# Hymba streaming step on one core: attention values as a two-part product, the first half of the output product placed between attention tiles, and an earlier order of the second state-space group

## Chip, core and metric

One core of a Trainium2 chip. The metric is device microseconds (us) of one execution of the whole two-layer step; lower is better. The engines are TensorE (PE in the rows, with its weight loads as PEld), VectorE (DVE), ScalarE (ACT), GpSimd (POOL) and SyncE (SP, which issues the DMAs).

## Reference

Each of two layers computes, for 1024 prompt tokens and 64 sample tokens, `h = RMSNorm(x)`, one combined projection `h . W_in`, three branches (A: a gated linear recurrence; B: attention over the top keys of an indexer; C: a Mamba-2 state-space scan in two groups), and `x + W_out . concat[y_A, y_B, y_C]`. All of it is float32. The part that matters here is B's tail and the output product:

```python
    p = jax.nn.softmax(logits, axis=-1)
    o = jnp.einsum('bqgrk,bqkgd->bqgrd', p.astype(vsel.dtype), vsel)
...
    y_b = o * jax.nn.silu(ga)
...
    mix = jnp.concatenate([y_a, y_b, y_c], axis=-1)
    x = x + jnp.einsum('bte,ed->btd', mix, p['w_out'].astype(mix.dtype)).astype(x.dtype)
```

The kernel masks the keys that the indexer did not choose instead of gathering the chosen ones, so the softmax and the product with V run over all keys up to the query's tile.

## The kernel before, in words

**Numbers in two parts.** Most products are made of float32 split into a high part (type fp32r) and a low part (the rest): `three` (lines 212 to 217) makes hi.hi, hi.lo and lo.hi, one matmul per part and per 128 rows of depth. `split` (188 to 194) makes the parts of a 128x1024 weight block: ScalarE the high, VectorE or GpSimd the low.

**Attention** (966 to 1122). Work is cut into 18 tiles per layer, list `todo` (1110): a tile of 128 queries (64 for tile 8, the sample tokens) for one of two key-value groups of four heads. Tile t < 8 sees 128(t+1) keys; tile 8 sees 576. The loop at 1115 starts the queries of tile i+2, the weights of tile i+1 and the values of tile i. `weigh` (1038) per head: two matmuls per 512 keys (1068), VectorE adds mask and bias while it takes a running extreme (1071), ScalarE takes the exponential with its sum (1075), VectorE the reciprocal (1077) and the normalized weights (1078). `values` (1081) per block of 128 keys: four transposes of the weights into one bank (1093), a ScalarE copy to `pT` (1095), and for each pair of heads a float32 matmul with 64 columns of V (1098) into the one bank `s1`; at the end VectorE multiplies with the gate (1100) and two DMAs write `ybd` (1102). A layer has 82 such blocks: 72 of 128 queries and 10 of tile 8.

**Output product.** `out_proj` (956 to 964) goes over eight blocks d of 128 output rows; each has three chunks of columns, 24 matmuls a chunk. Its first half (1127) needs `yad` and the first state-space group and no attention; it is written after the attention loop in the program, and it is what TensorE has to do beside attention. Its second half (1161, 1165) needs `ybd`: chunks 0 and 1 hold tokens of tiles 0 to 5, chunk 2 those of tiles 6 to 8. `y_tile` (942) loads a piece and splits it; line 1158 does so for all three chunks before line 1161.

**Order.** The framework lays out a fixed order for every engine from the order of the program and a simulated clock; an engine then runs its list in order. Work later in the program has lower priority and fills gaps. `PLAN` (22) is a list written by hand of projections (x, z, a, q, l, g) and steps of the two state-space groups (s0, s1); `run(PLAN[3])` at 927 and `steps(g[1])` at 928 end the stage before attention. Each s1 is one tile of the second group (`ssd`, 747); after its last tile come token sums, a norm (817) and the write of `ycd` (819). l and g are the recurrence blocks and their gates.

**Memory.** The attention's constant tiles (`kst`, `vt`, `nb`, `ks`) lie where the state-space pools lay and wait until those are free; then `nb` (971), `vt` (980 to 982) and `ks` (988) are loaded by SP, in order. Two banks `tp` hold transposes, three `mm` the output product, one `s1` the values.

Of the kernel before, what the change touches and what calls it, by code (L numbers as in the profile page):

```python
# [20 lines left out]
DEPTH = 2  # L21
PLAN = ('', 'X8 x10 z2 x1 x0 z3 x2 x3 s0 x9 s0 z4 s0 x11 s0 z5 s0 z6 s0 x4 s0 X5 s0 z7 s0 s0 X6 x7', 's0 s1 a0 q1 s0 q0 s1 a1', 's1 s1 q3 q2 s1 l0 s1 g0 s1 l1 g1 s1 s1 l2 g2 s1 l3 s1 g3', 'a3 a2')
RAW = 2
# [14 lines left out]
TS = 64  # L38
# [44 lines left out]
def body(ctx, tc, I, O):  # L83
# [36 lines left out]
    def s1_bank():  # L120
        return bank("s1", 1)
# [42 lines left out]
    def softplus(out, x, n, tag, sign=1.0, where=None):  # L164
# [16 lines left out]
        V.scalar_tensor_tensor(out, q, 2.0, z, op0=OP.mult, op1=OP.add)  # L181

    def load(block):
        raw = wts.tile([128, 1024], F32, name="wraw", bufs=RB)
        SP.dma_start(raw, block)
        return raw

    def split(raw, eng):

        hi = wts.tile([128, 1024], F32R, name="whi")  # L190
        lo = wts.tile([128, 1024], F32R, name="wlo")
        S.activation(hi, raw, AF.Copy)  # L192
        eng.tensor_tensor(lo, raw, hi.bitcast(F32), op=OP.subtract)  # L193
        return hi.rearrange("p (k c) -> p k c", k=8), lo.rearrange("p (k c) -> p k c", k=8)
# [84 lines left out]
    for l in range(DEPTH):  # L279
# [675 lines left out]

        def out_proj(half, Y, chunks, done, eng=G):

            for d in range(8):
                ws = weights(I["w_out"][l, half, d], eng)
                for ci in chunks:  # L960
                    a, b = CH[ci]
                    ps = mm_bank()
                    three(ps[:, :b - a], ws, Y, ci)
# [15 lines left out]

        SP.dma_start(vt[:, 0:8, :], kvd[:, 0:8, 128:256])  # L980
        SP.dma_start(vt[:, 8:12, :], I["cache_att_v"][l])
        SP.dma_start(vt[:TS, 12, :], kvd[:TS, 8, 128:256])
        kf, kc_ = [p.tile([128, 1024], F32, name="lg", bufs=8) for _ in range(2)]
# [5 lines left out]
        def keys(g, t0, w):  # L989

            n = TS if t0 == 12 else 128
            kb_ = (ks_ if t0 == 12 else kf)[:n, t0 % 12:t0 % 12 + w, 64 * g:64 * g + 64][:, :, None, :].to_broadcast([n, w, 2, 64])
            khl = p.tile([128, 2, 4, 64], F32R, name="pT")
            S.activation(khl[:n, :w, 0:2, :], kb_, AF.Copy)
# [43 lines left out]
        def weigh(t, g, qst):  # L1038
# [15 lines left out]
            for h in range(4):  # L1054
# [22 lines left out]
                V.reciprocal(ri[:nq, h:h + 1], sm[:nq, h:h + 1])  # L1077
                V.tensor_scalar(lg[:nq, :nk], lg[:nq, :nk], ri[:nq, h:h + 1], None, op0=OP.mult)  # L1078
            return lgs

        def values(t, g, lgs):

            nq = rows_of(t)
            nk = reach(t)[1]
            ga = p.tile([128, 2, 128], F32, name="ga", bufs=1)
            SP.dma_start(ga[:, :, :nq], gad[:, 2 * g:2 * g + 2, t * 128:t * 128 + nq])
            av = s1_bank()[:, :256].rearrange("p (r q) -> p r q", r=2)
            nb_ = (nk + 127) // 128
            for j in range(nb_):
                n = min(128, nk - 128 * j)  # L1090
                ps = tp_bank()
                for i, h in enumerate((0, 2, 1, 3)):
                    PE.transpose(ps[:n, i * nq:(i + 1) * nq], lgs[h][:nq, j * 128:j * 128 + n], ident[:nq, :nq])  # L1093
                pT = p.tile([128, 4, 128], F32, name="pT")
                S.activation(pT[:n, :, :nq], ps[:n, :4 * nq].rearrange("p (r q) -> p r q", r=4), AF.Copy)  # L1095
# [17 lines left out]
        run(PLAN[4])  # L1113
        all_keys(1)
        for i, (t, g_) in enumerate(todo):
            if i + 2 < len(todo):
# [18 lines left out]
        def add_last(d, ci, a, b, ps):  # L1135
# [6 lines left out]
            SP.dma_start(x_, xd[d][:, a:b])  # L1142
            V.tensor_tensor(x_, x_, ps[:, :w], op=OP.add)  # L1143
            if not last:
# [89 lines left out]
```

## Time and profile before

| | us |
|---|---|
| median of 3 runs | 2049.99 |
| lowest and highest | 2048.08, 2056.05 |
| the profiled execution: its time | 2043.88 |
| its span, first to last instruction | 2042.1 |
| TensorE busy | 1952.6 (96%) |
| VectorE busy | 1519.2 (74%) |
| ScalarE busy | 1231.8 (60%) |
| GpSimd busy | 651.2 (32%) |

A busy share is an average over stages. Matmuls are pipelined: the time that one takes away from the next is read from the distance of two starts, not from its duration. The attention stages lie at about 680 to 957 us (layer 1) and 1690 to 1960 us (layer 2).

### The profile page before, as it was taken

Reading aid. Unit: us, or ns where it says so; the run is one execution under the profiler, and the core shown is the slowest. Engines: PE = TensorE matmul, PEld = TensorE weight load, DVE = VectorE, ACT = ScalarE, POOL = GpSimd, SP = SyncE. Lnnn points to the kernel's source line nnn. Section 1 sums busy time; section 2 is a strip of 40 time slices with the busy share of each in tenths; the row PEclk is TensorE's granted clock in tenths of the full one; section 3 lists DMA queues with packets and bytes.
Section 4 is the critical chain, followed back from the end, with each engine's and each line's share of the span. In section 5 each row is a group of like instructions: output and inputs, shape, how many; then the busy total and the mean of one; then the engine's idle time right before and its main releaser. Section 6 shows DMA issues by size and latency. Waiting matters only on the chain.

```text
span 2042.1 us, 34620 instructions
## 1 busy us (share of the span) xinstructions
PE 1952.6 (96%) x12056; PEld 1747.9 (86%) x12056; DVE 1519.2 (74%) x3701; ACT 1231.8 (60%) x2567; POOL 651.2 (32%) x561
## 2 busy tenths in 40 slices
PE   6999999989999899999999999999899999999999
PEld 5899989888889787866998999999888887888589
DVE  7778899898866855574386888999987678566723
ACT  6569988753656544454355798987446655444621
POOL 3012244333522422253430213353245224223320
PEclk9999999999999899999999999999999998999999
DMA  6125354535332732324541343545353346234145
GB/s 228 62 72 143 101 167 123 173 105 154 107 109 83 231 116 89 106 89 137 191 134 38 108 124 108 161 137 165 99 163 97 96 149 197 90 99 140 46 145 169
DMA packets 252079, 257.94 MB, mean 126 GB/s; under 512 B 31264, under 2 KB 230304, under 8 KB 251904
## 3 DMA queue, kind: packets, MB, share of 16 engines
q1 hardware_dynamic: 251904, 255.73, 40.9%
q8 instruction: 95, 1.56, 0.3%
q14 instruction: 80, 0.66, 0.1%
HBM read 181.09 MB, written 74.57 MB: 125 GB/s over the span
## 4 chain that ended last, share of the span: by engine, by line
PE 66%; DVE 19%; DMA 6%; ACT 5%; issue 3%; SPq 1%; POOL 0%; DVEq 0%; ACTq 0%
PE mm L216 16%; PE mm L215 15%; PE mm L217 15%; PE s L1098 4%; PE tp L1093 4%; PE s L1068 3%; DVE u L855 2%; ACT junka L580 2%; PE s L881 1%; DMA cumB<-cumd 1%; PE s L514 1%; DMA eB<-cumd 1%; ACT cumB L742 1%; DMA xsc<-xsd 1%; PE s L791 1%
## 5 line engine op out<-in xcount | busy, mean ns | idle before, releaser
L193 POOL TENSOR_TENSOR wlo<-wraw,whi 128x1024 fp32r<-128x1024 f32 x80 | 195.4, 2442 | 364.0 <-ACT whi L192 360.3
L580 ACT ACTIVATE junka<-sc,cand 128x768 bf16<-128x768 f32 x248 | 239.4, 968 | 8.5 <-DVE sc L583 3.9
L192 ACT ACTIVATE whi<-wraw 128x1024 fp32r<-128x1024 f32 x130 | 137.1, 1054 | 135.3 <-PE mm L216 109.8
L1075 ACT ACTIVATE lg<-lg,mx 128x512 f32<-128x512 f32 (+8 forms) x144 | 111.2, 773 | 95.7 <-DVE mx L1071 95.3
L855 DVE SCALAR_TENSOR_TENSOR u<-raw,parh,u 128x384 f32<-128x384 f32 (+1 forms) x198 | 147.4, 751 | 11.7 <-POOL u L853 5.9
L1095 ACT ACTIVATE pT<-tp 128x512 f32<-128x512 f32 (+1 forms) x164 | 90.5, 568 | 108.1 <-PE tp L1093 103.5
L1060 POOL TENSOR_TENSOR nbm<-nb,shared 128x256 f32<-128x256 f32 (+1 forms) x112 | 81.2, 730 | 224.1 <-DVE mx L1071 201.8
L574 DVE TENSOR_SCALAR_CACHE_REDUCE junk<-sc,cand 128x384 bf16<-128x384 f32 (+4 forms) x194 | 139.9, 753 | 1.0
L1068 PE MATMUL s<-kst,qst 128*128 128x512 f32 (+4 forms) x448 | 120.8, 362 | 7.8 <-DVE mx L1071 7.3
L742 ACT ACTIVATE cumB<-cumB,ctk 128x128 f32<-128x128 f32 (+1 forms) x288 | 88.4, 384 | 54.3 <-DMA cumB<-cumd 47.7
L1093 PEld LDWEIGHTS tp<-identr,lg 128*128 128x128 f32 (+2 forms) x656 | 71.8, 140 | 45.6 <-issue 39.4
L1093 PE MATMUL tp<-identr,lg 128*128 128x128 f32 (+2 forms) x656 | 107.2, 278 | 0.5 <-DVE lg L1078 0.5
L1098 PE MATMUL s<-pT,vt 128*64 128x256 f32 (+2 forms) x656 | 104.8, 389 | 1.6 <-ACT pT L1095 1.6
L1078 DVE TENSOR_SCALAR lg<-lg,ri 128x512 f32<-128x512 f32 (+8 forms) x144 | 93.6, 651 | 3.3
L1143 DVE TENSOR_TENSOR xl<-xl,mm 128x384 f32<-128x384 f32 (+1 forms) x40 | 21.4, 540 | 94.1 <-PE mm L217 84.9
L1068 PEld LDWEIGHTS s<-kst,qst 128*128 128x128 f32 (+1 forms) x448 | 72.2, 188 | 21.9 <-DVE mx L1071 13.4
L215 PE MATMUL mm<-sth0a,whi 128*128 128x384 f32 (+1 forms) x228 | 82.9, 365 | 7.3 <-DVE xl L1143 2.0
L1071 DVE CUSTOM_DVE_ANT_0 lg<-s,shared 128x512 f32<-128x512 f32 (+4 forms) x112 | 61.8, 553 | 37.7 <-PE s L1068 31.9
L193 DVE TENSOR_TENSOR wlo<-wraw,whi 128x1024 fp32r<-128x1024 f32 x50 | 64.1, 1281 | 32.1 <-ACT whi L192 32.0
L216 PE MATMUL mm<-stl1a,whi 128*128 128x384 f32 (+1 forms) x228 | 79.6, 349 | 3.8 <-DVE stl1a L954 3.5
L216 PE MATMUL mm<-stl0a,whi 128*128 128x384 f32 (+1 forms) x228 | 79.8, 350 | 2.4 <-POOL stl0a L954 2.0
L778 POOL TENSOR_TENSOR hT<-hT,dec 128x512 f32<-128x512 f32 x28 | 35.9, 1282 | 144.3 <-DVE hT L780 137.0
(475 smaller groups left out, 6931.1 us busy)
## 6 DMA issues: line engine op xcount, KB each, us to landing
wraw<-in_w_in_dram SPq DMA_DIRECT2D x82, 512.0 KB, 3.5
wraw<-in_w_out_dram SPq DMA_DIRECT2D x48, 512.0 KB, 3.8
cumB<-cumd SPq DMA_DIRECT2D x32, 512.0 KB, 4.8
xsd<-u SPq DMA_DIRECT2D x48, 192.0 KB, 2.4
gz<-gzd SPq DMA_DIRECT2D x32, 256.0 KB, 3.6
xsc<-xsd SPq DMA_DIRECT2D x32, 256.0 KB, 3.5
eB<-cumd SPq DMA_DIRECT2D x56, 128.0 KB, 4.1
gzd<-g SPq DMA_DIRECT2D x32, 192.0 KB, 1.9
```

What stands on the lines that cost most here:

```text
L192: S.activation(hi, raw, AF.Copy)
L193: eng.tensor_tensor(lo, raw, hi.bitcast(F32), op=OP.subtract)
L215: PE.matmul(ps, hi[:, k, :], xh[ci][:, c0:], start=k == 0, stop=False)
L216: PE.matmul(ps, hi[:, k, :], xl[ci][:, c0:], start=False, stop=False)
L217: PE.matmul(ps, lo[:, k, :], xh[ci][:, c0:], start=False, stop=k == len(xs) - 1)
L574: V.tensor_scalar(junk, sc[j][:n], thr, None, op0=op, op1=OP.add, accum_out=out)
L580: S.activation(junk, sc[j][:n], AF.Sign, scale=-1.0, bias=cand, accum_out=out)
L855: V.scalar_tensor_tensor(u, raw[:, j:j + n], w[:, wbase + j * wstride:wbase + j * wstride + 1], u, op0=OP.mult, op1=OP.add)
L1068: PE.matmul(ps[:nq, :b - a], qst[:, h, :nq], kst[:, g, pt, kbase + a:kbase + b], start=pt == 0, stop=pt == 1)
L1075: S.activation(lg[:nq, :nk], lg[:nq, :nk], AF.Exp, scale=-1.0, bias=mx[:nq, h, k_ - 1:k_], accum_out=sm[:nq, h:h + 1])
L1093: PE.transpose(ps[:n, i * nq:(i + 1) * nq], lgs[h][:nq, j * 128:j * 128 + n], ident[:nq, :nq])
L1098: PE.matmul(av[64 * b:64 * b + 64, :, :nq], vt[:n, vj, 64 * g:64 * g + 64], pT[:n, 2 * b:2 * b + 2, :nq], start=j == 0, stop=j == nb_ - 1)
```

## The change

Values: V is split once per layer into `vhl`, with 64 high and 64 low columns side by side; the transposed weights are split into a high part `pT` (ScalarE) and a low part `pl` (VectorE). Each block makes two matmuls over all 128 columns and four heads, and at the end of a tile the two halves of the result are copied across partitions and added. The normalization of heads 1 and 3 goes from VectorE to ScalarE. The matmuls of block d of the output product's first half are placed, in TensorE's order, behind the value matmul at which (d-1)/8 of the layer's keys are done (blocks 0 and 1 are free). Chunk 2 of the second half's pieces is made inside the second half, behind block 2. Four of the nine s1 steps of `PLAN[3]` stand earlier; none is left beside l2, g2, l3, g3.

`tc.issue_after(x)` puts the instructions made inside it that run on x's engine behind x in that engine's order.

```diff
-PLAN = (..., 's1 s1 q3 q2 s1 l0 s1 g0 s1 l1 g1 s1 s1 l2 g2 s1 l3 s1 g3', 'a3 a2')
+PLAN = (..., 's1 s1 q3 s1 q2 s1 l0 s1 g0 s1 l1 s1 g1 s1 s1 l2 g2 l3 g3', 'a3 a2')
...
-        vt = kp.tile([128, 13, 128], F32, name="vt")
+        vhl = kp.tile([128, 13, 2, 128], F32R, name="vhl")
...
+        v0, v1 = [p.tile([128, 1024], F32, name="lg", bufs=8) for _ in range(2)]
...
+            S.activation(vhl[:n, a:b, :, 0:64], v, AF.Copy)
+            G.tensor_tensor(vhl[:n, a:b, :, 64:128], v, vhl[:n, a:b, :, 0:64].bitcast(F32), op=OP.subtract)
...
-                V.tensor_scalar(lg[:nq, :nk], lg[:nq, :nk], ri[:nq, h:h + 1], None, op0=OP.mult)
+                if h % 2:
+                    S.activation(lg[:nq, :nk], lg[:nq, :nk], AF.Copy, scale=ri[:nq, h:h + 1])
+                else:
+                    V.tensor_scalar(lg[:nq, :nk], lg[:nq, :nk], ri[:nq, h:h + 1], None, op0=OP.mult)
...
+                pT = p.tile([128, 4, 128], F32R, name="pT", bufs=3)
+                pl = p.tile([128, 4, 128], F32R, name="pl")
+                S.activation(pT[:n, :, :nq], ps, AF.Copy)
+                V.tensor_tensor(pl[:n, :, :nq], ps, pT[:n, :, :nq].bitcast(F32), op=OP.subtract)
...
-                for b in range(2):
-                    PE.matmul(av[64 * b:64 * b + 64, :, :nq], vt[:n, vj, 64 * g:64 * g + 64], pT[:n, 2 * b:2 * b + 2, :nq],
-                              start=j == 0, stop=j == nb_ - 1)
-            V.scalar_tensor_tensor(ga[:, :, :nq], av[:, :, :nq], 0.5, ga[:, :, :nq], op0=OP.mult, op1=OP.mult)
+                for k_, w in enumerate((pT, pl)):
+                    marks["av"] = PE.matmul(av[:, :, :nq], vhl[:n, vj, g, :], w[:n, :, :nq], start=j == 0 and k_ == 0,
+                              stop=j == nb_ - 1 and k_ == 1)
+            sm2 = p.tile([128, 2, 128], F32, name="sm2", bufs=1)
+            S.activation(sm2[0:64, :, :nq], av[64:128, 0:2, :nq], AF.Copy)
+            S.activation(sm2[64:128, :, :nq], av[0:64, 2:4, :nq], AF.Copy)
+            for b in range(2):
+                c = slice(64 * b, 64 * b + 64)
+                V.tensor_tensor(sm2[c, :, :nq], sm2[c, :, :nq], av[c, 2 * b:2 * b + 2, :nq], op=OP.add)
+            V.scalar_tensor_tensor(ga[:, :, :nq], sm2[:, :, :nq], 0.5, ga[:, :, :nq], op0=OP.mult, op1=OP.mult)
...
+            work += reach(t)[1]
+            done_.append((work, marks["av"]))
...
-        out_proj(0, Y, (0, 1, 2), add_x, EA)
+        def behind(d):
+            ins = [m for w, m in done_ if w <= work * (d - 1) / 8]
+            return tc.issue_after(ins[-1].ins) if ins else ExitStack()
+        out_proj(0, Y, (0, 1, 2), add_x, EA, behind)
...
-        for ci in range(3):
+        for ci in range(2):
             for k in range(8):
-                y_tile(Y, srcs, k, ci, ci == 2)
-        out_proj(1, Y, (0, 1), add_last, EB)
+                y_tile(Y, srcs, k, ci)
+        def add_early(d, ci, a, b, ps):
+            add_last(d, ci, a, b, ps)
+            if d == 2 and ci == 1:
+                with tc.issue_after(marks["split"].ins), tc.issue_after(marks["xl"].ins):
+                    for k in range(8):
+                        y_tile(Y, srcs, k, 2, True)
+        out_proj(1, Y, (0, 1), add_early, EB)
```

`marks["split"]` is the last ScalarE split of a weight block, `marks["xl"]` VectorE's last add in the second half.

## Rows read from the trace of the kernel before

**Rows 1.** The page: span, busy shares, the 40 slices of TensorE.
```profile
span 2042.1 us, 34620 instructions
...
PE 1952.6 (96%) x12056; PEld 1747.9 (86%) x12056; DVE 1519.2 (74%) x3701; ACT 1231.8 (60%) x2567; POOL 651.2 (32%) x561
...
PE   6999999989999899999999999999899999999999
```

**Rows 2.** Windows by stage: stretch, length, busy per engine, PEclk, DMA share, GB/s.
```profile
660.00:680.00 20.00, 15.67 (x91) 13.92 (x90) 13.89 (x40) 6.77 (x14) 6.56 (x4) 0.89 0.82 265
...
680.00:700.00 20.00, 17.36 (x82) 15.00 (x81) 17.35 (x57) 12.19 (x36) 10.17 (x11) 0.68 0.68 220
700.00:880.00 180.00, 180.00 (x1145) 145.80 (x1144) 108.16 (x351) 87.60 (x186) 56.45 (x59) 1.00 0.39 120
880.00:950.00 70.00, 65.12 (x401) 40.84 (x400) 44.59 (x142) 40.80 (x80) 24.27 (x24) 1.00 0.19 55
950.00:1000.00 50.00, 50.00 (x290) 50.00 (x289) 9.42 (x16) 12.95 (x20) 25.41 (x18) 1.00 0.63 199
1680.00:1720.00 40.00, 33.37 (x170) 28.27 (x172) 34.90 (x101) 22.35 (x62) 22.77 (x22) 0.74 0.70 217
1720.00:1880.00 160.00, 160.00 (x1030) 133.02 (x1027) 94.39 (x303) 75.17 (x158) 43.51 (x46) 1.00 0.36 110
1880.00:1957.00 77.00, 70.52 (x436) 45.12 (x435) 52.03 (x154) 44.89 (x89) 28.07 (x29) 1.00 0.24 72
```

**Rows 3.** Timeline of TensorE in layer 1's tail: start, duration of the group, instructions.
```profile
916.38 0.65 PE L1098 MATMUL s<-pT,vt 128*64 128x256 f32 x4
916.97 0.66 PE L1093 MATMUL tp<-identr,lg 128*128 128x128 f32 x4
917.38 0.60 PE L1068 MATMUL s<-kst,qst 128*128 128x384 f32 x2
917.91 0.65 PE L1098 MATMUL s<-pT,vt 128*64 128x256 f32 x4
918.49 0.66 PE L1093 MATMUL tp<-identr,lg 128*128 128x128 f32 x4
918.90 0.71 PE L1068 MATMUL s<-kst,qst 128*128 128x512 f32 x2
919.55 0.65 PE L1098 MATMUL s<-pT,vt 128*64 128x256 f32 x4
```

**Rows 4.** Chain of waits, layer 1's last tile: start, length of the step, what.
```profile
941.59 0.58 PE s L1098 x4
942.17 0.59 PE tp L1093 x4
942.76 0.58 PE s L1098 x4
943.34 0.59 PE tp L1093 x4
```

**Rows 5.** Timeline of TensorE where fp32r score matmuls stand between output matmuls.
```profile
782.12 0.63 PE L1068 MATMUL s<-kst,qst 128*128 128x512 f32 x2
782.58 0.34 PE L216 MATMUL mm<-stl2a,whi 128*128 128x384 f32 x1
782.76 0.34 PE L217 MATMUL mm<-sth2a,wlo 128*128 128x384 f32 x1
```

**Rows 6.** VectorE and ScalarE by line and form: busy, mean ns of one, idle before.
```profile
L780 DVE TENSOR_TENSOR hT<-hT,s 128x512 f32<-128x512 f32 x32 | 21.7, 678 | 1.7 <-PE s L773 1.4 <-PE tp L731 0.3
...
L1100 DVE SCALAR_TENSOR_TENSOR ga<-s,ga 128x256 f32<-128x256 f32 x32 | 13.4, 420 | 28.5 <-PE s L1098 24.7 <-DMA ga<-gad 2.9 <-DMA qn<-qnd 0.6
...
L1095 ACT ACTIVATE pT<-tp 128x512 f32<-128x512 f32 x144 | 83.2, 594 | 94.2 <-PE tp L1093 90.0 <-PE s L1068 2.4 <-PE s L1098 0.9
...
L1095 ACT ACTIVATE pT<-tp 128x256 f32<-128x256 f32 x16 | 5.8, 383 | 10.7 <-PE tp L1093 10.5
```

**Rows 7.** The page, groups by cost: exponentials and normalization.
```profile
L1075 ACT ACTIVATE lg<-lg,mx 128x512 f32<-128x512 f32 (+8 forms) x144 | 111.2, 773 | 95.7 <-DVE mx L1071 95.3
...
L1078 DVE TENSOR_SCALAR lg<-lg,ri 128x512 f32<-128x512 f32 (+8 forms) x144 | 93.6, 651 | 3.3
```

**Rows 8.** Line 1107 (first half's add): duration min/median/max, first and last start.
```profile
L1107 DVE TENSOR_TENSOR g<-g,mm x48: 471/548/555, 706.7 to 1881.2; 128x384 f32<-128x384 f32 x32, 128x320 f32<-128x320 f32 x16
```

**Rows 9.** Chain of waits at the start of layer 2's attention.
```profile
1677.04 1.01 DVE yC L817 x2
...
1680.63 0.33 SPq L971
...
1683.11 6.62 DMA ks<-kvd
1689.82 0.32 ACT pT L994
```

More of the change, by code (lines that the diff above doesn't have):

```diff
@@ L21 @@
 DEPTH = 2
[L22 removed]
+PLAN = ('', 'X8 x10 z2 x1 x0 z3 x2 x3 s0 x9 s0 z4 s0 x11 s0 z5 s0 z6 s0 x4 s0 X5 s0 z7 s0 s0 X6 x7', 's0 s1 a0 q1 s0 q0 s1 a1', 's1 s1 q3 s1 q2 s1 l0 s1 g0 s1 l1 s1 g1 s1 s1 l2 g2 l3 g3', 'a3 a2')
 RAW = 2
@@ L181, in softplus @@
         V.scalar_tensor_tensor(out, q, 2.0, z, op0=OP.mult, op1=OP.add)
+    marks = {}
     def load(block):
@@ L191, in split @@
         lo = wts.tile([128, 1024], F32R, name="wlo")
-        S.activation(hi, raw, AF.Copy)
+        marks["split"] = S.activation(hi, raw, AF.Copy)
         eng.tensor_tensor(lo, raw, hi.bitcast(F32), op=OP.subtract)
@@ L954, in y_tile, with out_proj @@
             (V if k % 8 in YL else G).tensor_tensor(Y[k][1][ci], s_, Y[k][0][ci].bitcast(F32), op=OP.subtract)
-        def out_proj(half, Y, chunks, done, eng=G):
+        def out_proj(half, Y, chunks, done, eng=G, behind=None):
             for d in range(8):
@@ L962, in out_proj @@
                     ps = mm_bank()
-                    three(ps[:, :b - a], ws, Y, ci)
+                    with behind(d) if behind else ExitStack():
+                        three(ps[:, :b - a], ws, Y, ci)
                     done(d, ci, a, b, ps)
         kst = kp.tile([128, 2, 2, TP + PAST + TS], F32R, name="kst")
-        vt = kp.tile([128, 13, 128], F32, name="vt")
+        vhl = kp.tile([128, 13, 2, 128], F32R, name="vhl")
         def near_bias(g):
@@ L978, in body @@
         nb = near_bias(0)
-        SP.dma_start(vt[:, 0:8, :], kvd[:, 0:8, 128:256])
-        SP.dma_start(vt[:, 8:12, :], I["cache_att_v"][l])
-        SP.dma_start(vt[:TS, 12, :], kvd[:TS, 8, 128:256])
+        v0, v1 = [p.tile([128, 1024], F32, name="lg", bufs=8) for _ in range(2)]
+        v0, v1 = [v.rearrange("p (t c) -> p t c", c=128) for v in (v0, v1)]
+        SP.dma_start(v0, kvd[:, 0:8, 128:256])
+        SP.dma_start(v1[:, 0:4, :], I["cache_att_v"][l])
+        SP.dma_start(v1[:TS, 4, :], kvd[:TS, 8, 128:256])
+        for v, n, a, b, c in ((v0, 128, 0, 8, 0), (v1, 128, 8, 12, 0), (v1, TS, 12, 13, 4)):
+            v = v[:n, c:c + b - a].rearrange("p t (g c) -> p t g c", g=2)
+            S.activation(vhl[:n, a:b, :, 0:64], v, AF.Copy)
+            G.tensor_tensor(vhl[:n, a:b, :, 64:128], v, vhl[:n, a:b, :, 0:64].bitcast(F32), op=OP.subtract)
         kf, kc_ = [p.tile([128, 1024], F32, name="lg", bufs=8) for _ in range(2)]
@@ L992, in keys @@
             kb_ = (ks_ if t0 == 12 else kf)[:n, t0 % 12:t0 % 12 + w, 64 * g:64 * g + 64][:, :, None, :].to_broadcast([n, w, 2, 64])
-            khl = p.tile([128, 2, 4, 64], F32R, name="pT")
+            khl = p.tile([128, 2, 4, 64], F32R, name="pT", bufs=3)
             S.activation(khl[:n, :w, 0:2, :], kb_, AF.Copy)
@@ L1086, in values @@
             SP.dma_start(ga[:, :, :nq], gad[:, 2 * g:2 * g + 2, t * 128:t * 128 + nq])
-            av = s1_bank()[:, :256].rearrange("p (r q) -> p r q", r=2)
+            av = s1_bank().rearrange("p (r q) -> p r q", r=4)
             nb_ = (nk + 127) // 128
@@ L1093, in values @@
                     PE.transpose(ps[:n, i * nq:(i + 1) * nq], lgs[h][:nq, j * 128:j * 128 + n], ident[:nq, :nq])
[L1094 to L1100 removed]
+                ps = ps[:n, :4 * nq].rearrange("p (r q) -> p r q", r=4)
+                pT = p.tile([128, 4, 128], F32R, name="pT", bufs=3)
+                pl = p.tile([128, 4, 128], F32R, name="pl")
+                S.activation(pT[:n, :, :nq], ps, AF.Copy)
+                V.tensor_tensor(pl[:n, :, :nq], ps, pT[:n, :, :nq].bitcast(F32), op=OP.subtract)
+                vj = j + (8 if t == 8 else 0)
+                for k_, w in enumerate((pT, pl)):
[8 more added lines that the diff above has]
+            V.scalar_tensor_tensor(ga[:, :, :nq], sm2[:, :, :nq], 0.5, ga[:, :, :nq], op0=OP.mult, op1=OP.mult)
             for i in range(2):
@@ L1114, in body @@
         all_keys(1)
+        work, done_ = 0, []
         for i, (t, g_) in enumerate(todo):
@@ L1142, in add_last @@
             SP.dma_start(x_, xd[d][:, a:b])
-            V.tensor_tensor(x_, x_, ps[:, :w], op=OP.add)
+            marks["xl"] = V.tensor_tensor(x_, x_, ps[:, :w], op=OP.add)
             if not last:
```

## The prediction

> **What bounds it now.** I read the page first: TensorE is busy 96% of the span, VectorE 74%, ScalarE 60% [rows 1]. So a saving must shorten TensorE's list or close its gaps, and the gaps are worth 90 us at most. Next, windows by stage [rows 2]. With the output product's first half beside attention, TensorE is busy 180 of 180 us and 160 of 160 us. Then that work is used up: its last add in layer 2 starts at 1881.2 [rows 8]. In the two tails, 880 to 950 and 1880 to 1957, TensorE is idle 4.9 and 6.5 us, and weight loads fall from 81% to 58% of the time: short instructions of attention alone. From 950 on, in the second half, it is full again, so there is nothing to gain there. At the start of attention it is idle 4.3 + 2.6 us (660 to 700) and 6.6 us (1680 to 1720) at a granted clock of 0.89, 0.68 and 0.74.
>
> Then the timeline in a tail, by distances of starts [rows 3]: TensorE goes from values to transposes to scores with hardly a gap. A values block takes 0.59 us (916.38 to 916.97). Four transposes take 0.41 us ahead of scores (916.97 to 917.38), but 0.59 us ahead of values (942.17 to 942.76) [rows 4]: the step into the 64-column matmuls costs up to 0.18 us more. At the end of a tile one block of transposes and values takes 1.17 us (941.59 to 942.76), all of it on the chain of waits [rows 4].
>
> **Values on TensorE.** Removed per block: four instructions, 0.58 us and the step into them. Added: two fp32r matmuls of 512 columns at full width. Their nearest row is a pair of score matmuls of that size between output matmuls: 0.46 us (782.12 to 782.58) [rows 5]. At worst they cost what such a pair took between transposes and values, 0.65 us (918.90 to 919.55) [rows 3]. So a block changes by +0.07 us at worst and by 0.58 + 0.18 - 0.46 = -0.30 us at best. I take -0.22 us, with 0.10 us for the step, since not every block stands straight behind transposes: 144 blocks, 32 us. The 20 blocks of tile 8 are half as wide; no row of their own is used, so their change lies between 0 and -0.30 us, and I take -0.2 us: 4 us. Together -36 us of TensorE, bounds +10 and -49 us.
>
> The Trainium skill, "TensorEngine Tiling (Array Packing)", section Key Properties, says that a change of tiling mode drains TensorE. By it the step would vanish wherever it is paid, and with the whole 0.18 us the sum would be 12 us better (164 x 0.08) than with my 0.10 us; the 0.59 against 0.41 us agree that it is paid.
>
> **What it costs the other engines, per layer.** VectorE gets the low part `pl` from a bank: the nearest row, an operation of this size with a bank as input, takes 678 ns [rows 6]; 72 x 0.68 + 10 x 0.42 = 53 us. The 36 adds of halves at no more than 0.42 us (the gate's multiply) [rows 6] are 15 us. Half of the normalization goes: a quarter of 93.6 us [rows 7] for one layer, 23 us. Net +45 us. From 680 to 950 VectorE is busy 17.4 + 108.2 + 44.6 = 170 us [rows 2]; 215 us in a stage that is to last about 250 is 86%. ScalarE, 141 us there [rows 2], gets 36 normalizations at about the exponential's 0.77 us [rows 7], 36 half copies at 0.38 us [rows 6] and 2 us for `vhl`: 185 us, 74%. GpSimd's three subtractions for `vhl` are work that no values matmul needs in its first microseconds; it is busy 56 of 180 us [rows 2], and I cost them at nothing. Neither engine becomes the bound on average. But TensorE runs its list in order, and the second matmul of a block now waits for ScalarE's copy and then VectorE's `pl`, behind which scores' adds (1071) and the even heads' normalization queue. A `tp` bank is held for 0.41 + 0.59 + 0.68 us plus two hand-overs, about 1.9 us; with two banks a block can follow every 0.95 us, under the 1.17 us of today. I let three quarters of the saving through: **-27 us**, bounds +10 and -49.
>
> **First half between the tiles.** A block d is 72 matmuls at up to 0.18 us (782.58 to 782.76) [rows 5], at most 13 us. Blocks 6 and 7, some 25 us, may start only at 5/8 and 6/8 of the keys, so they lie in or near the tail. Their work is only moved: what can be won is the idle time of the two tails, 11.4 us [rows 2]; what can be lost is as much again where the body then lacks filling. I take about half of it: **-6 us**. The output product's loads and splits are not held back, only its matmuls; its adds and SP's loads and stores for them come later with them, in a stage where DMA is busy 0.19 to 0.39 [rows 2].
>
> **State-space tiles earlier.** In layer 2 the last norm (817) at 1677.0 is followed on SP by `ycd`, three loads of `yad`, `nb`, the three loads of V, and `ks`, issued at 1683.1 and landed 6.6 us later; only then do keys go on (1689.8) [rows 9]. These loads wait for the memory of the state-space pools. With no s1 beside l2, g2, l3 and g3 that memory is free while those projections still fill TensorE. The idle time of the two starts is 13.5 us, and the lower clock costs 0.11 x 20 + 0.32 x 20 + 0.26 x 40 = 19 us [rows 2], so 32 us is the most. It can also lose: the recurrence blocks then stand with less beside them, and V's split takes 2 us of ScalarE a layer ahead of the keys. I take **-8 us**, bounds +8 and -32.
>
> **End of a tile.** The one `s1` bank was free after one operation of 0.42 us; now after two half copies and two adds, 0.38 + 0.38 + 0.42 + 0.42 = 1.6 us [rows 6], before the next tile's values may write it. That is +1.2 us for 36 tiles, 43 us, where nothing covers it; scores and transposes of the next tile and the first half's matmuls stand between. I take **+5 us**, bounds 0 and 43.
>
> **Chunk 2 inside the second half.** Nothing: TensorE is busy 50 of 50 us there [rows 2]. If SP's queue stood behind these eight loads (two buffers), the weight blocks would come late; they are loaded two ahead.
>
> **Sum:** 2043.9 - 27 - 6 - 8 + 5 = 2008 us for an execution like the profiled one. The median of the runs shown lies 6.1 us above that execution, so I forecast **2014 us**.
>
> **Rivals.** (a) Starts and tails close almost wholly as well: the full 36 us, 10 of the 11 and half of the 32, 62 us with nothing lost: 1988. For it speaks that TensorE is the chain nearly throughout; against it VectorE's 86%. (b) VectorE's queue sets the pace: if `pl` waits for one more operation of 0.68 us, a bank is held 2.6 us and a block takes 1.3 us, more than 1.17. The values' saving is then lost, and 2050 - 6 - 8 + 5 = 2041 remains. For it: VectorE was busy 64% of the tail already [rows 2]. (c) Slower: the `s1` bank. If ScalarE's exponentials (up to three of 0.77 us) stand ahead of the half copies, it is held some 2 us longer per tile with TensorE's next value matmul first in line: 36 x 1.6 = 58 us against the 36 won, 2072. It decides from 1 us per tile on. Against it: today's first value matmul of a tile stands behind scores, and the order is laid out with these operations known. (d) The packing of two 64-column tiles is worth more than the step: were the new matmuls to take 2 x 0.58 us, 164 blocks would lose 95 us, 2050 + 95 - 9 = 2136. The pair at 0.46 us [rows 5] speaks against it. The Trainium skill, "TensorEngine Tiling (Array Packing)", section Theoretical Speedup, gives up to 2x for 64 columns or fewer, which the change gives up; the instructions of rows 3 show what the old form really took.
>
> **How the numbers follow.** Forecast 0.60, with a range of its own of 1992 to 2034; (a) 0.12; (b) 0.16; (c) 0.11; (d) 0.01. The range from 1986 to 2044 takes in (a) and most of (b), and leaves out (c), (d) and the edges. A measurement of this kernel tells about 0.5%, 10 us, from no change. Faster by more than that (under 2039.7): the forecast, (a) and almost half of (b): 0.79. Within it: the rest of (b) and a little of (c): 0.11. Slower: 0.10.
>
> **What would show it.** In the changed kernel: values at about 0.46 us per block by starts, and transposes at 0.41 us whatever follows; TensorE's busy time down by some 30 us; matmuls of the output product until the end of the attention loop; `ks` landed before the last gate's matmuls end, and a granted clock near 1.00 at the start of attention; VectorE at 80% or more from 680 to 930. It is wrong if TensorE stands in front of value matmuls waiting for `pl` or for the add of halves, if the body between 700 and 880 now shows idle time that the tail's filling doesn't make good, or if the start of attention waits for the recurrence instead.

## The result and the profile after

The changed kernel takes **2060.2 us** (median of 9 runs, 2058.2 to 2070.6) against 2048.1 us before in the same runs: ratio 1.0060, 95% interval 1.0047 to 1.0074. It is 12 us slower, where 2014 us and a range up to 2044 had been forecast. The profiled execution took 2070.6 us, 10 us over its own median; so single numbers of it are compared stage by stage, and totals by medians.

The page of the changed kernel, span, busy shares and the slices of TensorE, to be read against [rows 1]:
```profile
span 2068.6 us, 34209 instructions
...
PE 1940.7 (94%) x11728; PEld 1781.4 (86%) x11728; DVE 1593.0 (77%) x3865; ACT 1306.4 (63%) x2717; POOL 647.5 (31%) x567
...
PE   6999999989899899998999999999999988999999
```
TensorE is lighter, by 11.9 us and not by the 30 forecast. VectorE has 73.8 us more, ScalarE 74.6. The span less TensorE's busy time was 89.5 us and is 127.9: TensorE now waits.

Windows of the changed kernel by stage, columns as in [rows 2]:
```profile
660.00:680.00 20.00, 18.03 (x109) 17.45 (x108) 11.80 (x24) 7.78 (x17) 8.08 (x6) 0.96 0.85 277
680.00:700.00 20.00, 15.88 (x88) 14.66 (x87) 18.45 (x48) 12.19 (x35) 8.96 (x8) 0.70 0.64 194
700.00:880.00 180.00, 172.00 (x1030) 148.74 (x1029) 141.69 (x447) 120.86 (x263) 53.36 (x60) 1.00 0.34 105
880.00:950.00 70.00, 65.46 (x360) 55.71 (x358) 53.24 (x133) 42.59 (x77) 24.88 (x22) 0.95 0.35 106
950.00:1000.00 50.00, 47.33 (x258) 47.33 (x259) 11.62 (x23) 13.45 (x23) 27.56 (x21) 0.93 0.63 202
1720.00:1880.00 160.00, 150.80 (x896) 130.69 (x895) 124.80 (x394) 105.38 (x233) 49.26 (x52) 0.99 0.37 110
1880.00:1957.00 77.00, 73.80 (x431) 64.60 (x430) 60.14 (x174) 48.95 (x95) 27.11 (x29) 0.98 0.32 97
```
The place to look at is the body of each attention stage (700 to 880 and 1720 to 1880). Before, TensorE was busy 180 of 180 and 160 of 160 us there [rows 2]; now 8.0 and 9.2 us are idle. VectorE went from 60% to 79% of the body (108.2 to 141.7 of 180 us), and in the tail of layer 1 to 76%.

The waits of TensorE in layer 1's attention (686 to 952) in the changed kernel; columns: engine, tile and line, what it waited for, us in total, times, longest:
```profile
PE s L1077 <- DVE mx L1080: 3.3, 6, 1.0
PE s L1113 <- DVE pl L1110: 2.2, 10, 0.4
PE tp L1105 <- ACT lg L1088: 2.1, 2, 1.1
PE s L1113 <- DVE sm L1121: 1.8, 2, 0.9
```
Line 1113 is the value matmuls. The waits for `pl` and for the add of halves (1121) are new, as is the one for a normalization on ScalarE (1088). No single one is large.

Timeline of TensorE in layer 1's last tiles, changed kernel:
```profile
932.28 0.39 PE L1113 MATMUL s<-pT,vhl 128*128 128x512 f32 x1
932.50 0.34 PE L218 MATMUL mm<-stl7a,whi 128*128 128x384 f32 x1
...
932.86 0.40 PE L1113 MATMUL s<-pl,vhl 128*128 128x512 f32 x1
933.10 0.60 PE L1105 MATMUL tp<-identr,lg 128*128 128x128 f32 x4
933.45 0.48 PE L1113 MATMUL s<-pT,vhl 128*128 128x512 f32 x1
933.77 0.39 PE L1113 MATMUL s<-pl,vhl 128*128 128x512 f32 x1
...
935.48 0.33 PE L1105 MATMUL tp<-identr,lg 128*128 128x128 f32 x1 [0.98 <-ACT lg L1088]
...
939.02 0.77 PE L1113 MATMUL s<-pT,vhl 128*128 128x512 f32 x1 [0.86 <-DVE sm L1121]
939.59 0.63 PE L1113 MATMUL s<-pl,vhl 128*128 128x512 f32 x1
940.01 0.63 PE L1113 MATMUL s<-pT,vhl 128*128 128x512 f32 x1
```
Where nothing waits, the pair of value matmuls takes 0.22 + 0.24 us (932.28 to 932.50, 932.86 to 933.10): the forecast's 0.46. Four transposes ahead of values take 0.35 us (933.10 to 933.45), where they took 0.59 [rows 4]. That is TensorE's gain, as argued. Then come the waits, and after two of them the matmuls follow each other at 0.42 us instead of 0.23. By distances of starts over 690 to 945, the new pair takes 0.63 us per block (mean spacing 0.317 us); the four old matmuls took 0.61 (0.153), and the step into them some 0.10 more. So of 0.25 us a block that the prices promise, 0.17 went into waits and into the lower clock behind them.

### The profile page after: what moved, and what is told of

Same layout as the page of the kernel before. It is cut to its first block, busy times and chain, and to the rows that moved or that the text cites. A ratio compares the mean times of both kernels' runs of the same rounds, so it can differ in the third digit from the quotient of the medians.

```text
span 2068.6 us, 34209 instructions
## 1 busy us (share of the span) xinstructions
PE 1940.7 (94%) x11728; PEld 1781.4 (86%) x11728; DVE 1593.0 (77%) x3865; ACT 1306.4 (63%) x2717; POOL 647.5 (31%) x567
## 5 line engine op out<-in xcount | busy, mean ns | idle before, releaser
L1069 POOL TENSOR_TENSOR nbm<-nb,shared 128x256 f32<-128x256 f32 (+1 forms) x112 | 76.4, 687 | 277.0 <-DVE mx L1080 231.0
L857 DVE SCALAR_TENSOR_TENSOR u<-raw,parh,u 128x384 f32<-128x384 f32 (+1 forms) x198 | 141.1, 718 | 17.2 <-POOL u L855 9.5
L1110 DVE TENSOR_TENSOR pl<-tp,pT 128x512 fp32r<-128x512 f32 (+1 forms) x164 | 106.1, 653 | 32.6 <-ACT pT L1109 31.3
L1109 ACT ACTIVATE pT<-tp 128x512 fp32r<-128x512 f32 (+1 forms) x164 | 89.8, 564 | 58.3 <-PE tp L1105 56.6
L1105 PEld LDWEIGHTS tp<-identr,lg 128*128 128x128 f32 (+2 forms) x656 | 80.3, 142 | 23.8 <-ACT lg L1088 4.1
L219 PE MATMUL mm<-sth2a,wlo 128*128 128x384 f32 (+1 forms) x228 | 80.0, 351 | 0.0
L219 PE MATMUL mm<-sth4a,wlo 128*128 128x384 f32 (+1 forms) x228 | 78.7, 345 | 0.0
L219 PE MATMUL mm<-sth0a,wlo 128*128 128x384 f32 (+1 forms) x228 | 78.1, 343 | 0.5 <-DVE wlo L195 0.5
```

Of the source, the lines that this page charges most:

```text
L219: PE.matmul(ps, lo[:, k, :], xh[ci][:, c0:], start=False, stop=k == len(xs) - 1)
L857: V.scalar_tensor_tensor(u, raw[:, j:j + n], w[:, wbase + j * wstride:wbase + j * wstride + 1], u, op0=OP.mult, op1=OP.add)
L1110: V.tensor_tensor(pl[:n, :, :nq], ps, pT[:n, :, :nq].bitcast(F32), op=OP.subtract)
```

## The experiments

All ratios are to the kernel before on the same chip, with their 95% intervals. **A** is the time from the first score matmul of a layer to the end of its last gate, **S** the time from the end of the top-key selection to that first score matmul (before: A 264.0 and 263.9, S 213.5 and 208.3 us in the two layers). Both are read from one execution each, and they trade: what a later start costs in S comes back in part in A, so two runs that differ in S are compared by S and A together.

### The parts alone

The new order of the state-space tiles alone:
```diff
-PLAN = (..., 's1 s1 q3 q2 s1 l0 s1 g0 s1 l1 g1 s1 s1 l2 g2 s1 l3 s1 g3', 'a3 a2')
+PLAN = (..., 's1 s1 q3 s1 q2 s1 l0 s1 g0 s1 l1 s1 g1 s1 s1 l2 g2 l3 g3', 'a3 a2')
```


> The kernel before with the changed PLAN alone. Theory PLAN (the earlier state-space tiles leave the last recurrence blocks without company, and the stage between the top-k search and attention gets longer): 2055 to 2062 us. Theory CHAIN (the two-part values put ScalarE's copy, VectorE's low part and the add of halves into TensorE's way, and take back there what they free; PLAN is neutral): 2043 to 2053 us. My forecast's own step: 2040 us.

0.9997 (0.9978 to 1.0016): nothing. S is shorter (208.4, 206.4) and A longer (265.5, 268.4): the gaps at the start are filled, and nothing ends earlier.

The values alone, with the split normalization; old order, first half and chunk 2 as before:
```diff
-out_proj(0, Y, (0, 1, 2), add_x, EA, behind)
+out_proj(0, Y, (0, 1, 2), add_x, EA)
...
```


> The kernel before with the two-part values alone (with the normalization of heads 1 and 3 on ScalarE), old PLAN, first half of the output product free, chunk 2 where it was. CHAIN: 2050 to 2070 us, the tails of the attention stages longer than in the changed kernel, because the output product's first half is used up before them. PLAN: 2020 to 2035 us, since the values free 36 us of TensorE.

1.0148 (1.0122 to 1.0175), 30 us slower. S is 225.9 and 220.9 us, some 12 more in each layer, and A 266.5 and 268.4, not shorter. The whole change with the old order:
```diff
-PLAN = (..., 's1 s1 q3 s1 q2 s1 l0 s1 g0 s1 l1 s1 g1 s1 s1 l2 g2 l3 g3', 'a3 a2')
+PLAN = (..., 's1 s1 q3 q2 s1 l0 s1 g0 s1 l1 g1 s1 s1 l2 g2 s1 l3 s1 g3', 'a3 a2')
```


> The changed kernel with the old PLAN. PLAN: 2044 to 2050 us, at least 10 us less than the changed kernel. CHAIN: 2056 to 2064 us, as the changed kernel.

1.0110 (1.0086 to 1.0133): the order that is worth nothing alone is worth 10 us beside the values. S is 222.7 and 224.8 here, 213.4 and 217.4 with the new order. A goes the other way, 259.4 and 259.6 here against 265.2 and 267.5, so the two profiles show 3 of the 10 us in S and A together.

The first half held back alone (`behind` added to the kernel before):
```diff
+            work += reach(t)[1]
+            done_.append((work, marks["av"]))
...
-out_proj(0, Y, (0, 1, 2), add_x, EA)
+out_proj(0, Y, (0, 1, 2), add_x, EA, behind)
...
```


> The kernel before with the first half of the output product held back to the attention tiles as in the change; old values, old PLAN. If the tails are short of filling: 2036 to 2044 us, with TensorE full up to the end of the attention loop. If holding it back only moves the idle time into the body: 2048 to 2056 us.

**0.9932 (0.9911 to 0.9953): 2037.8 us, 14 us faster.** Two windows of it:
```profile
700.00:880.00 180.00, 176.76 (x1146) 140.28 (x1144) 116.33 (x384) 91.88 (x203) 50.80 (x56) 0.99 0.33 100
880.00:950.00 70.00, 68.14 (x419) 51.48 (x418) 42.53 (x110) 36.00 (x66) 29.23 (x27) 1.00 0.38 114
```
The tail's idle time falls from 4.9 to 1.9 us, and the body pays 3.2 us. A is 260.7 and 262.0 instead of 264.0 and 263.9, so the profile shows about 5 of the 14 us.

### Where the start of attention went

V's loads behind K's and V's split behind the first tile's weights, in the changed kernel and in it with the old order:
```diff
-        SP.dma_start(v0, kvd[:, 0:8, 128:256])
...
         SP.dma_start(ks_[:TS, 0], kvd[:TS, 8, 0:128])
+        SP.dma_start(v0, kvd[:, 0:8, 128:256])
...
         ws_ = [weigh(*todo[0], qs[0])]
+        for v, n, a, b, c in ((v0, 128, 0, 8, 0), (v1, 128, 8, 12, 0), (v1, TS, 12, 13, 4)):
+            S.activation(vhl[:n, a:b, :, 0:64], v, AF.Copy)
```


> The changed kernel with V's loads behind those of K and V's split behind the first tile's weights in the program; nothing else. Theory START (V's three loads and its split stand ahead of the keys on SP and ScalarE, and wait for the same memory; this delays the first scores by some 10 us a layer): 2038 to 2048 us, first scores within 10 us of the last store of the recurrence. Theory CHAIN alone (the two-part values within the attention stage are the whole loss): 2056 to 2062 us, as the changed kernel.

> The same with the old PLAN. START: PLAN helped the changed kernel only because it freed the memory earlier for V's split ahead of the keys, so without that split in the way the old PLAN costs little: within 6 us of the run above, 2040 to 2052 us, instead of 14 us more. If PLAN is worth 14 us by itself in this company: 2054 to 2062 us.

1.0087 (1.0062 to 1.0111) and 1.0127 (1.0103 to 1.0151): no better than the same kernels with V first. S with the old order stays long, 219.5 and 221.6 us against 222.7 and 224.8 with V first. So V's loads and split account for 3 us a layer of the delay at most. SP's timeline of the second run points at something else:
```profile
673.17 0.38 SPq L974 DMA_DIRECT2D nb<-in_near_bias_dram  x1
673.64 0.38 SPq L985 DMA_DIRECT2D lg<-kvd  x1
674.07 0.81 SPq L986 DMA_DIRECT2D lg<-in_cache_att_k_dram  x1
```
K's load (985) is first behind `nb`, with no V ahead of it, and still goes out at 673.6 us. In the kernel before it went out 13 us ahead of `nb`, so its buffers lay in memory that was free by then:
```profile
660.25 0.39 SPq L985 DMA_DIRECT2D lg<-kvd  x1
...
673.70 0.38 SPq L971 DMA_DIRECT2D nb<-in_near_bias_dram  x1
```
The new tiles (a third copy buffer, `pl` twice, `sm2`: 7 KB a partition) make the pool larger, so that it would reach into what the state-space tiles hold. (`vhl` also takes 6.5 KB more than `vt`, in the pool of the constant tiles; that was not tested by itself.) To test the first, 7 KB that nobody uses, on the kernel with the first half held back and the old values:
```diff
+        bal = p.tile([128, 1792], F32, name="bal", bufs=1)
+        G.memset(bal[:, 0:1], 0.0)
```


> The kernel before with the first half held back (2038 us), and 7 KB a partition more in the pool that holds the attention's working tiles, about what the new values' third copy buffer, low parts and half sums take there; one GpSimd memset of one column is its only use. FOOTPRINT (a larger pool reaches down into memory that the state-space tiles give back late, so K's first loads and splits start later): the stretch from the top-key selection to the first scores grows by 5 to 10 us in each layer, and the run takes 2046 to 2058 us. SPLIT or LOADS (V's loads and split, or the new values' own work, make the start late): 2034 to 2042 us.

**1.0033 (1.0015 to 1.0051), 2059.3 us: 7 KB cost 1.0% (1.0033 against 0.9932), 21 us.** S goes from 212.5 and 211.3 to 224.3 and 219.0. Its SP timeline and the window behind it:
```profile
674.35 0.38 SPq L974 DMA_DIRECT2D nb<-in_near_bias_dram  x1
...
676.60 0.68 SPq L988 DMA_DIRECT2D lg<-kvd  x1
677.32 2.70 SPq L989 DMA_DIRECT2D lg<-in_cache_att_k_dram  x1
```
```profile
680.00:700.00 20.00, 13.20 (x66) 11.60 (x66) 14.04 (x31) 9.71 (x25) 8.55 (x9) 0.59 0.82 252
```
K's load is 16 us later than in the kernel before (660.25), and from 680 to 700 TensorE is busy 13.2 us at a granted clock of 0.59, where it had 17.4 at 0.68 [rows 2]. Unused memory is enough by itself to move the load and to cost the time; no value matmul was touched, and the memset takes 0.10 us. Where all of the 21 us go is not shown. S grows by 19.5 us over both layers, but A shrinks by 11.3 (253.8 and 257.6 against 260.7 and 262.0), so the late start shows 8. Another 10 us of the two profiles lie between the end of layer 1's attention and the end of layer 2's top-key selection (545.9 against 536.4 us), where nothing was edited. Of the whole change, the run with the old order and the one with the new order issue K's load at:
```profile
680.83 0.66 SPq L994 DMA_DIRECT2D lg<-kvd  x1
...
669.30 0.59 SPq L994 DMA_DIRECT2D lg<-kvd  x1
```
The earlier state-space tiles let it go out 11.5 us earlier. That fits the 10 us which the order is worth beside the values, but the 3 us in S and A together show only a part of them.

### What the low part costs

Both matmuls of a block read the high part, and `pl` is not made (the low part is left out; TensorE's work is the same):
```diff
-                V.tensor_tensor(pl[:n, :, :nq], ps, pT[:n, :, :nq].bitcast(F32), op=OP.subtract)
...
-                for k_, w in enumerate((pT, pl)):
+                for k_, w in enumerate((pT, pT)):
```


> The changed kernel without the low part: both matmuls of a block read the high part, and VectorE's subtraction is gone (the values count the high part twice and leave the low part out). TensorE's list is the same length, VectorE is 53 us a layer lighter and no matmul waits for it. CHAIN: 2005 to 2030 us, attention stages of about 245 us instead of 265. PLAN or a filler theory: 2045 us or more.

0.9954 (0.9936 to 0.9972), 2041.6 us. Then with `pl` made, and read by no matmul:
```diff
-                for k_, w in enumerate((pT, pl)):
+                for k_, w in enumerate((pT, pT)):
```


> The changed kernel, VectorE still makes the low part, but the second matmul of each block reads the high part again (the low part of the weights is left out of the values). TensorE no longer waits for the low part; VectorE's work and the time that a bank of transposes is held stay. Without VectorE's operation at all this kernel took 2042 us, with it and the wait 2060. If the wait of TensorE is the price: 2040 to 2046 us. If VectorE's load and the held bank are the price: 2054 to 2062 us.

1.0048 (1.0033 to 1.0064), 2062.7 us: as slow as the changed kernel. Making `pl` costs some 20 us whether or not a matmul reads it (4 KB of memory went with it; over both layers S differs by 4 us, A by 15). TensorE's waits in that run, 690 to 950:
```profile
PE tp L1105 <- DVE pl L1110: 2.3, 4, 0.8
PE s L1113 <- ACT pT L1109: 1.8, 4, 0.6
```
The wait has only moved, from the value matmul to the transposes, whose bank `pl` holds. So the bank was the next suspect. First three banks instead of two:
```diff
-        return bank("mm", 3)
+        return bank("mm", 2)
...
-        return bank("tp", 2)
+        return bank("tp", 3)
```


> The changed kernel with three banks for transposes and two for the output product, instead of two and three. Theory HELD (the low part's operation costs because it keeps one of the two transposes banks 0.7 us longer, so that the next block's transposes wait): most of the 20 us that the operation costs come back, 2040 to 2047 us. Theory QUEUE (it costs because VectorE's list is longer by it, and score adds, adds of halves and adds of the output product come later): a third bank changes little, 2055 to 2065 us. In between, or slower, if the output product with two banks waits for its adds: over 2065 us.

1.0282 (1.0262 to 1.0302). A is 266.4 and 265.6 against 265.2 and 267.5; the loss is elsewhere: S is 248.7 and 246.2, and layer 1's first score matmul comes 21 us later than in the changed kernel. The projections have one bank less there, which was not tested apart. This run tells little of the bank. Better: `pl` from the copy in memory, so that the bank is free after ScalarE (`pl` is then zero: the low part is left out), with the second matmul reading `pT`, then `pl`:
```diff
-                V.tensor_tensor(pl[:n, :, :nq], ps, pT[:n, :, :nq].bitcast(F32), op=OP.subtract)
+                V.tensor_tensor(pl[:n, :, :nq], pT[:n, :, :nq].bitcast(F32), pT[:n, :, :nq].bitcast(F32), op=OP.subtract)
```


> The changed kernel with the low part made from the copy in memory instead of the transposes bank (so it is zero: the low part is left out), and the second matmul reads the high part again. VectorE has as many operations as in the changed kernel; the bank is free after ScalarE's copy; no matmul waits for the low part. BANK or MATMUL (the price is what waits for the operation): 2038 to 2048 us, as with the operation taken away. QUEUE (the price is its time in VectorE's list): 2054 to 2064 us.

> As the run before it (low part from the copy in memory, so zero: left out), but the second matmul reads it, as in the changed kernel. BANK (the price is the transposes bank that is held until the low part is made): 2038 to 2048 us. MATMUL (TensorE's list stands behind the second matmul's wait): 2054 to 2064 us though the run before is faster. QUEUE: 2054 to 2064 us in both.

1.0095 (1.0077 to 1.0112) and 1.0092 (1.0075 to 1.0109): 2070.8 and 2070.4 us, both slower than the changed kernel. Freeing the bank and taking the matmul's wait away give nothing back. Two groups of the page of the first, GpSimd's mask add and VectorE's `pl`:
```profile
L1069 POOL TENSOR_TENSOR nbm<-nb,shared 128x256 f32<-128x256 f32 (+1 forms) x112 | 89.2, 801 | 260.1 <-DVE mx L1080 229.3
...
L1110 DVE TENSOR_TENSOR pl<-pT 128x512 fp32r<-128x512 f32 (+1 forms) x164 | 122.4, 759 | 20.3 <-ACT pT L1109 19.7
```
and the same two in the changed kernel:
```profile
L1069 POOL TENSOR_TENSOR nbm<-nb,shared 128x256 f32<-128x256 f32 (+1 forms) x112 | 76.4, 687 | 277.0 <-DVE mx L1080 231.0
...
L1110 DVE TENSOR_TENSOR pl<-tp,pT 128x512 fp32r<-128x512 f32 (+1 forms) x164 | 106.1, 653 | 32.6 <-ACT pT L1109 31.3
```
From memory `pl` takes 759 ns instead of 653: 16 us more of VectorE, and 10 us more of time (1.0095 against 1.0048 of the run with `pl` from the bank, unread). By elimination that leaves VectorE's list itself; the next two runs test it.

### The load on VectorE

All normalization on VectorE, as before the change; then that of heads 0 and 2 left out altogether:
```diff
-                if h % 2:
+                if False:
```
```diff
-                else:
-                    V.tensor_scalar(lg[:nq, :nk], lg[:nq, :nk], ri[:nq, h:h + 1], None, op0=OP.mult)
```


> The changed kernel with the normalization of all four heads on VectorE, as before the change. VectorE gets some 47 us more over the two layers, ScalarE is relieved of as much. QUEUE (VectorE's list sets the pace of attention): 10 to 25 us slower, 2070 to 2085 us. HELD, or ScalarE's list as the one that sets the pace: 2050 to 2062 us.

> The changed kernel without the normalization of heads 0 and 2 (it leaves that part of the computation out; heads 1 and 3 stay on ScalarE). VectorE is relieved of some 47 us over the two layers, and nothing else is touched: no bank, no matmul, no ScalarE operation. QUEUE: by the 20 us that 90 us of VectorE were worth with the low part, about 10 us faster, 2046 to 2054 us. HELD: 2057 to 2063 us.

1.0194 (1.0171 to 1.0218), 2087.3 us: 27 us slower than the changed kernel, though ScalarE was relieved. The other: 1.0047 (1.0030 to 1.0065), 2062.6 us, no gain against the changed kernel's 1.0060, where the theory of VectorE's list had forecast 2046 to 2054. So adding to VectorE's list cost time, and taking 43 us of work off it in A gave none back. Put the windows of A of five runs side by side (layer 1, then layer 2; columns as in [rows 2], VectorE's busy time is the third one behind the length). Without `pl`:
```profile
685.70:946.30 260.60, 244.42 (x1450) 215.64 (x1449) 165.20 (x536) 171.75 (x365) 86.96 (x88) 0.96 0.37 112
1695.70:1949.90 254.20, 241.91 (x1450) 214.84 (x1449) 162.52 (x536) 173.54 (x365) 87.38 (x88) 0.97 0.38 114
```
Without half of the normalization:
```profile
685.70:947.00 261.30, 246.97 (x1450) 213.91 (x1449) 186.30 (x582) 173.15 (x366) 83.19 (x88) 0.98 0.37 111
1694.80:1960.90 266.10, 248.82 (x1450) 215.78 (x1449) 184.01 (x582) 172.51 (x366) 84.10 (x88) 0.97 0.36 108
```
The changed kernel:
```profile
686.80:952.00 265.20, 249.06 (x1450) 215.19 (x1449) 208.57 (x618) 172.10 (x364) 84.43 (x88) 0.97 0.36 109
1713.00:1980.50 267.50, 249.39 (x1447) 214.25 (x1446) 204.71 (x616) 171.92 (x365) 83.73 (x87) 0.98 0.35 106
```
`pl` from memory, unread:
```profile
688.10:960.00 271.90, 248.45 (x1450) 217.66 (x1449) 220.74 (x619) 173.48 (x366) 91.30 (x88) 0.95 0.35 107
1708.70:1980.20 271.50, 250.42 (x1450) 220.10 (x1449) 214.23 (x619) 174.39 (x366) 91.34 (x88) 0.94 0.35 106
```
All normalization on VectorE:
```profile
687.70:965.90 278.20, 253.25 (x1450) 216.02 (x1449) 226.38 (x654) 149.24 (x330) 85.02 (x88) 0.97 0.34 104
1718.00:1995.90 277.90, 251.81 (x1450) 215.58 (x1449) 222.15 (x654) 149.29 (x330) 87.37 (x88) 0.97 0.35 104
```
VectorE's share of A (both layers) goes 64, 70, 78, 80, 81%, and A itself 515, 527, 533, 543, 556 us. In these five, which share the new order, A rises with VectorE's load, though VectorE never reaches 100%; ScalarE has least to do in the slowest, so it does not set this pace. In the slowest run TensorE's wait for `pl` in layer 1 is 8.1 us instead of 2.2. It is no law of the share. The whole change with the old order has VectorE at 78% too, and an A of 519 us (behind an S that is 17 us longer):
```profile
701.90:961.20 259.30, 244.73 (x1432) 211.79 (x1430) 203.04 (x609) 170.01 (x361) 79.89 (x83) 0.98 0.34 103
1722.70:1982.30 259.60, 241.75 (x1432) 208.02 (x1430) 201.35 (x608) 170.29 (x360) 79.53 (x83) 1.00 0.34 103
```
And the 527 of the run without half of the normalization comes from an execution 10 us under the median of its kernel, the 533 of the changed kernel from one 10 us over its own, so this difference is not to be leaned on. What is shown is the price of the operations: some 20 us for `pl`, 10 for its longer form, 27 for the normalization of heads 1 and 3 moved onto VectorE. That they cost it through VectorE's list is the reading that is left, with one run against it. One rival was not tested: the framework lays out every engine's order anew for each of these versions, so no two of them differ by an operation alone.

### Put together

Everything but the values, that is the new order, the first half held back and chunk 2 inside the second half, on the kernel before; then the same without the last of them:
```diff
-        out_proj(0, Y, (0, 1, 2), add_x, EA)
+        out_proj(0, Y, (0, 1, 2), add_x, EA, behind)
...
-        out_proj(1, Y, (0, 1), add_last, EB)
+        out_proj(1, Y, (0, 1), add_early, EB)
...
```


> The kernel before with everything of the change except the values: the first half of the output product held back to the tiles, the new order of the state-space tiles, chunk 2 inside the second half; values as 64-column float32 matmuls, all normalization on VectorE. If the parts add up by themselves (held back -13 us, order 0, chunk 2 nothing): 2033 to 2041 us, the fastest so far. If the new order gives something as soon as the body has less filling at the start of attention: 2020 to 2032 us. If chunk 2 inside the second half costs: over 2041 us.

> The kernel before with the first half of the output product held back and the new order of the state-space tiles; chunk 2 made ahead of the second half as before. If chunk 2 inside the second half is what took 8 us from the run without the values: 2034 to 2041 us. If it is the order, which is neutral alone but leaves less at the start of attention once the first half is held back: 2042 to 2050 us.

0.9981 (0.9968 to 0.9994) and 0.9982 (0.9970 to 0.9995). Chunk 2 inside the second half is worth nothing, and the new order takes back some 10 us of what holding back the first half gained. A is longer with it (263.2 and 263.2; 264.1 and 266.3; against 260.7 and 262.0). Why it costs this much, with S shorter by 1 to 3 us a layer, was not settled.

The new values in seven of 18 tiles, V split for one group at a time from `vt` behind the first tile, on the kernel with the first half held back:
```diff
-            values(t, g_, ws_[i])
+            (values2 if i in range(3, 17, 2) else values)(t, g_, ws_[i])
```


> The kernel before with the first half held back, and seven of the 18 tiles of a layer (every second from the fourth on) with values as products of two parts; V is split for one group at a time, behind the first tile and ahead of the ninth, so nothing stands ahead of the first keys; normalization on VectorE. Seven tiles hold some 32 of 82 blocks, 64 over both layers: 64 x 0.22 = 14 us of TensorE. If VectorE's slack carries the low parts where they stand apart: 2026 to 2035 us. If the block's chain costs as much wherever it stands: 2036 to 2050 us.

1.0061 (1.0041 to 1.0081), 2064.0 us. K's load goes out at 674.17 us, right behind `nb` and `vt`, and S is 221.4 and 219.6: the sign of memory again, with nothing of V's split ahead of the keys. Last, the normalization's split with the old values and the first half held back:
```diff
+                if h % 2:
+                    S.activation(lg[:nq, :nk], lg[:nq, :nk], AF.Copy, scale=ri[:nq, h:h + 1])
+                else:
                     V.tensor_scalar(lg[:nq, :nk], lg[:nq, :nk], ri[:nq, h:h + 1], None, op0=OP.mult)
```


> The kernel before with the first half held back, and the normalization of heads 1 and 3 on ScalarE; values as before. With the old values TensorE is the bound of attention and VectorE is at some 65%. If taking 47 us off VectorE shortens the few waits for score adds (5.5 us over both layers): 2031 to 2037 us. If it changes nothing: 2035 to 2041 us. If ScalarE's copies of the transposes now wait behind the normalization, as a block's first step: over 2041 us.

0.9938 (0.9919 to 0.9957), 2038.6 us: the split changes nothing there. The fastest version found is the kernel before with its first half held back, with or without this split: by the ratios 13 to 14 us under the kernel before and 25 to 26 under the changed one.

## Why the prediction was wrong

**What bounds it.** TensorE did bound the kernel before, and the new values did shorten its list. But the bound was read as staying there: "neither engine becomes the bound on average" was true of the average and wrong as a conclusion. With VectorE at 78% of A, the low part's operation lengthens the run by 20 us.

**Values on TensorE (-27).** The prices held: 0.46 us for a pair, 0.35 us for the transposes, and the step into the 64-column form 0.09 us behind a matmul of the output product and 0.17 us behind transposes (below). The trace agrees with the rule of the Trainium skill, "TensorEngine Tiling (Array Packing)", section Key Properties, that a change of tiling mode drains TensorE: with the 64-column matmuls gone, so is the step. (With the whole step the prediction's sum would be 13 us better by its 164 x 0.08, not 12.) What failed is "I let three quarters of the saving through". Measured against everything but the values (0.9981), the changed kernel (1.0060) says that the values cost 16 us in its company, where -27 was forecast. Of the 43 us between the two, the low part's operation is some 20; without it the kernel took 2042 us (0.9954), some 6 us less than everything but the values. So even without the low part three quarters did not come through: over both layers TensorE is idle 28.5 us of A there, against 13.5 without the values. What those 15 us wait for was not tested apart. The bank arithmetic (held 1.9 us, a block every 0.95 us) was the wrong question: freeing the bank early gained nothing.

**First half between the tiles (-6).** Right in sign and place, and too small: -14 alone. It was masked in the whole.

**State-space tiles earlier (-8).** This step failed too. It costed V's split (2 us of ScalarE), and V's place turned out to matter little; it never asked how much memory the new tiles take and when that memory comes free, although [rows 9] was read as "these loads wait for the memory". 7 unused KB cost 21 us with the old order and the old values. The new order is neutral alone, costs 10 us beside the held-back first half and is worth 10 beside the values, where K's load goes out 11.5 us earlier with it; S in the changed kernel is no shorter than before.

**End of a tile (+5).** About right: 3.9 us of TensorE's waits over both layers are for the add of halves, without the lower clock behind them.

**Chunk 2 (0).** Right.

**Sum.** Step by step, by ratios: the values alone +30 us, the first half and chunk 2 beside them -8, the order -10: +12. (The first half is worth 14 alone and 8 beside the values.) Memory had no term in the forecast's sum; it is 21 us in the run with unused bytes, and was not measured alone in the changed kernel. The low part's operation had 9 us, the quarter of the saving that was not let through, and costs 20.

**Rivals.** (b), VectorE's queue sets the pace, came nearest, though one run speaks against it; its price was capped at the values' saving, so its 2041 lay under what came. (c) named the wrong wait. The list of signs of being wrong came true: idle time in the body, a granted clock of 0.70 from 680 to 700, VectorE at 79% from 680 to 950 (18.45 + 141.69 + 53.24 of 270).

## What to carry to other kernels

Count the bytes that a change adds to a pool, and ask which load's buffers they push into memory that comes free late: here 7 unused KB cost as much as 164 operations of 0.65 us. When work moves from the bounding engine to one that is busy 60 to 65%, do not take room in its average for room in time: here the run grew while that engine stood at 78%. Test the operation's price by leaving it out and by leaving it in unread. Run the parts of a change alone: one of these was worth 14 us and was buried under the other.

## What the runs showed of the hardware

- **The step into 64-column float32 matmuls.** In the kernel before, the distance from an output matmul of 384 columns to the next matmul is 0.174 us, and 0.267 us where that is a value matmul (40 places of the full width); from the last transpose it is 0.028 us, and 0.202 us ahead of values (the median of 26 places). In the changed kernel the same distances are 0.173 and 0.028 us.
- **A subtraction on memory alone is slower, and GpSimd's adds are longer beside it.** VectorE's subtraction takes 653 ns with the bank as one input, and 759 and 748 ns in the two runs with memory for both; GpSimd's mask adds take 801 and 772 ns in those two, and 687 to 739 ns in the others.
- **The granted clock in the tail.** Windows of the changed kernel:
```profile
935.00:939.00 4.00, 2.31 (x11) 1.40 (x12) 2.22 (x5) 3.18 (x7) 0.00 (x0) 0.85 0.40 131
939.00:944.00 5.00, 4.97 (x16) 4.04 (x16) 2.32 (x4) 1.03 (x3) 0.00 (x0) 0.50 0.25 63
```
After 4 us in which TensorE was busy 2.31, the next 5 us ran at the lower clock (1.2 GHz), value matmuls at 0.42 us instead of 0.23: the two waits of 1.84 us cost up to 2.5 us more behind them.
